# The token-major copy of x: whole transfers out, pieces of 512 bytes back, and a copy on ScalarE

## The chip, the cores and the metric

The kernel runs on one core of a Trainium2 chip. Its metric is the device time of one execution in microseconds (us); the time before is the median of three runs, 964.47 us. Work is spread over five engines that run side by side and wait for each other by semaphores: TensorE (PE, matrix products), VectorE (DVE), ScalarE (ACT), GpSimd (POOL) and SyncE (SP, which issues transfers). Transfers between device memory (DRAM) and the on-chip memory run on 16 DMA engines. Those that SP issues go into one queue (q1 in the profile), those that POOL issues into another (q0).

## The reference

Two decoder layers over 256 tokens of 1024 features, and a last normalization. Only the last block of layer 1, a feed-forward block, and the final normalization matter here:

```python
def rmsnorm(x, g):
    y = x32 * lax.rsqrt(jnp.mean(x32 * x32, axis=-1, keepdims=True) + EPS)
    return y.astype(x.dtype) * g

def swiglu(x, w_gate, w_up, w_down):
    return (jax.nn.silu(x @ w_gate) * (x @ w_up)) @ w_down

...
    x = x + 0.5 * swiglu(rmsnorm(x, ffn2_norm[l]), ffn2_w_gate[l], ffn2_w_up[l], ffn2_w_down[l])
return rmsnorm(x, final_norm)
```

w_gate and w_up are 1024 x 2816, w_down is 2816 x 1024. Everything is float32.

## The kernel before

**Stream of weights.** All weights come as one stream of 1 MB loads into four `raw` buffers (L117, issued by SP). PE multiplies float32 as a high and a low part, so each half of a load (a block of 128 x 1024) is split: ACT writes the high part `whi` (L143), DVE the low part `wlo` (L144). There are five buffers of each. A load can only be issued when its raw buffer, the one used four loads before, has been split; a block can only be split when PE is through with the block five before. Every product with a tile of weights is three matmuls (L579 to L581 for gate and up, L688 to L690 for a group that is made with seven products in the place of eight, L795 to L797 for the last down projection).

**x and its copy.** The residual x lies in on-chip memory with features on the partitions: a tile of 128 partitions x 8 feature groups x 256 tokens. The last block puts out tokens on the partitions, so it needs x turned. This is done through a DRAM tile `tok`, while PE works on gate and up. `to_tokens` (L508) is called four times, for two feature groups each: DVE transposes blocks of 32 x 32 (L513) into a tile `q`, and SP issues eight DMAs (L516) that put the pieces in their places of `tok`, which is 256 tokens x 1024 features. A run of 32 features is a piece, 128 bytes; a DMA moves 32 partitions x 8 pieces. `from_tokens` (L840) reads all of `tok` back with one DMA from POOL's queue (L842) into the tile `bias`, 128 partitions x 2 token halves x 1024 features, which `evac_tok` (L804) then uses: it adds half the down projection to it, takes the mean of squares, scales it, and the result goes out from there.

**What else runs there.** The hidden values are turned by `turned_back` (L544): POOL writes a tile `v`, `kT` or `k` to DRAM (L551) and reads it back with four DMAs (L553); ACT and DVE split what comes back into `h` (L561, L562). For the group with seven products, 1 MB loads with accumulation go from POOL's queue into the tiles `k2` and `bias` (L536, L633), and blocks are split from these too.

**Order.** `Order` (L200) holds a planned time of PE in nanoseconds; `pe.after(delay, fn, 0)` places `fn` at that planned time, in the order of the program. `to_tokens` is placed 16, 25, 34 and 43 us after the block's start, `from_tokens` 88 us after it. Each engine carries out its instructions in that order. SP holds the loads and the tok writes in one line, ACT the splits, the activations and everything else that is given to it.

Of the kernel before, what the change touches and what calls it, by code (L numbers as in the profile page):

```python
# [15 lines left out]
F32 = mybir.dt.float32  # L16
F32R = mybir.dt.float32r
AF = mybir.ActivationFunctionType
# [5 lines left out]
P = 128  # L24
D = 1024
KT = D // P
S = 256
# [213 lines left out]
def paired(t):  # L241

    return t.rearrange("p (b a) -> p a b", b=2)
# [22 lines left out]
def build(nc, tc, ctx, a):  # L266
    consts = ctx.enter_context(tc.tile_pool(name="consts", bufs=1))
    wpool = ctx.enter_context(tc.tile_pool(name="wpool", bufs=1))
    act = ctx.enter_context(tc.tile_pool(name="act", bufs=1))
    psum = ctx.enter_context(tc.tile_pool(name="psum", bufs=1, space=PSUM))  # L270
    dram = ctx.enter_context(tc.tile_pool(name="dram", bufs=1, space=DRAM))
# [13 lines left out]
    def w2():  # L285
        return act.tile([P, 512], F32, name="w2", bufs=6)
# [5 lines left out]
    x = consts.tile([P, KT, S], F32, name="x")  # L292
# [22 lines left out]
    pe = Order()  # L315
# [192 lines left out]
    def to_tokens(tok, k):  # L508


        to = tok.rearrange("(c i) (k p j) -> p k i c j", i=32, p=4, j=32)
        t = act.tile([P, 2 * S], F32, name="q2", bufs=2)
        tc.keep_in_program_order(nc.vector.transpose(t, x[:, k:k + 2].rearrange("p k s -> p (k s)")))  # L513
        for p in range(4):
            for i in range(2):
                tc.keep_in_program_order(nc.sync.dma_start(  # L516
                    to[p, k + i], t[32 * p:32 * p + 32, i * S:(i + 1) * S].rearrange("i (c j) -> i c j", j=32)))


    def placed(at):  # L520
        return [at + o // 2 + i for i, o in enumerate(PLACES)]
# [16 lines left out]
    def ffn(which, layer, n, nxt, first=False, last=False):  # L538
# [206 lines left out]
        def have(ks):  # L745
            return lambda: math.inf if any(h[k] is None for k in ks) else 0.0
# [26 lines left out]
        def down_tok():  # L773

            late = 2 * (ws.BUFS - 1)
            pss, got, mean = {}, {}, [EPS, EPS]

            def part(fs, *regions):  # L780

                c = regions[0][1] // 512

                def go():
                    for f in fs:
                        if (f, c) not in got:
                            got[f, c] = ws.take(f"{which}_w_down", layer, f * P, c * 512, 4)
                        for reg in regions:
                            u, c0, c1 = reg
                            if f == 0:  # L790
                                pss[reg] = (sc_tile if c == 1 and c1 - c0 == 512 else acc_tile)()[:, :c1 - c0]
                            ps = pss[reg]
                            wh, wl = (paired(w)[:, (c0 - c * 512) // 2:(c1 - c * 512) // 2] for w in got[f, c])
                            hh, hl = (h[f].v[:, u, m] for m in range(2))
                            nc.tensor.matmul(ps, hh, wh, start=f == 0, stop=False)  # L795
                            nc.tensor.matmul(ps, hh, wl, start=False, stop=False)  # L796
                            nc.tensor.matmul(ps, hl, wh, start=False, stop=f == FT - 1)  # L797
                    if fs[-1] == FT - 1:
                        for u, c0, c1 in regions:
                            evac_tok(u, slice(c0, c1), pss[u, c0, c1])  # L800

                return have(fs), go, sum(len(fs) * (c1 - c0) * 654 // 512 for _, c0, c1 in regions)

            def evac_tok(u, at, ps):  # L804
                xtok = back["x"]
                y = xtok[:, u, at]
                g = gfin[at.start // 512][:, at.start % 512:at.start % 512 + at.stop - at.start]
                nc.vector.scalar_tensor_tensor(y, ps, 0.5, y, op0=ALU.mult, op1=ALU.add)
                ms = act.tile([P, 1], F32, name="mean", bufs=4)
                junk = w2()[:, :at.stop - at.start]  # L810
                nc.vector.tensor_tensor_reduce(junk, y, y, 1.0 / D, mean[u], ALU.mult, ALU.add, ms)
                mean[u] = ms
                if at.stop < D:
                    nc.gpsimd.tensor_tensor(y, y, g, op=ALU.mult)
                    return
                r = act.tile([P, 1], F32, name="rcol", bufs=2)
                nc.gpsimd.tensor_tensor(r, ms, mhalf[:, 0:1], op=ALU.pow)
                nc.vector.tensor_tensor(y, y, g, op=ALU.mult)
                out = a["out"][u * P:(u + 1) * P]
                cuts = (0, 384, 704, D)  # L820
                nc.scalar.activation(xtok[:, u, :cuts[1]], xtok[:, u, :cuts[1]], AF.Copy, scale=r)
                nc.scalar.dma_start(out[:, :cuts[1]], xtok[:, u, :cuts[1]])
                for i, j in zip(cuts[1:], cuts[2:]):
                    nc.vector.tensor_scalar(xtok[:, u, i:j], xtok[:, u, i:j], r, None, op0=ALU.mult)
                    nc.sync.dma_start(out[:, i:j], xtok[:, u, i:j])

            end = range(FT - late, FT)
            right = ((0, 512, D), (1, 512, 768), (1, 768, D))
            return [part(range(i, i + 2), (0, 0, 512), (1, 0, 512)) for i in range(0, FT, 2)] + [
                part(range(FT - late), *right)] + [part(end, reg) for reg in right]  # L830
# [4 lines left out]
        norm_scale(n, 18900 if first else 2300, unpin=True, turn=not first, wide=False)  # L835
        if last:
            gfin = []
            tok, back = dram.tile([S, D], F32, name="tok"), {}

            def from_tokens():  # L840
                back["x"] = t = act.tile([P, 2, D], F32, name="bias", bufs=1)
                tc.keep_in_program_order(nc.gpsimd.dma_start(t, tok.rearrange("(u q) f -> q u f", u=2)))  # L842

            def last_factors():
                gfin.extend(act.tile([P, 512], F32, name="p2", bufs=4) for _ in range(2))
                src = a["final_norm"]
                for i, g in enumerate(gfin):
                    nc.sync.dma_start(g, bass.AP(tensor=src.tensor, offset=src.offset + i * 512, ap=[[0, P], [1, 512]]))

            pe.after(90000, last_factors, 0)  # L850
            for k in range(0, KT, 2):
                pe.after(16000 + 9000 * (k // 2), lambda k=k: to_tokens(tok, k), 0)
            pe.after(88000, from_tokens, 0)
        at = AT.get((which, layer))
        groups = [f0 for f0 in range(0, FT, 4) if at is None or f0 != SEVEN]
        ups = [f for f0 in groups for f in hidden(f0)]
# [504 lines left out]
    pe.after(60000, mem_scale, 0)  # L1361
    pe.after(100000, lambda: early.update(bias=load_bias(0)), 0)
    ffn("ffn1", 0, n, nxt, first=True)
    bias, sinks = early["bias"], (vecs[:, VCOL["sinks"]:VCOL["sinks"] + 8], nsinks)

# [11 lines left out]
    memory(0, n, nxt, keys[0])  # L1377
    n, nxt = nxt, xn(("ffn1_norm", 1))
    ffn("ffn2", 0, n, nxt)
    n, nxt = nxt, xn(("mix_norm", 1))  # L1380
    pe.after(114000, lambda: early.update(bias=load_bias(1)), 0)
    ffn("ffn1", 1, n, nxt)
    n, nxt = nxt, xn(("xa_norm", 1))
    odd_mixer(n, nxt, early["bias"], mem_keys(1))
# [73 lines left out]
```

## Time and profile before

| | us |
|---|---|
| runs | 965.64, 964.47, 962.23 (median 964.47) |
| the profiled execution's own time | 963.72 |
| its span, first to last instruction | 961.9 |
| mean granted TensorE clock | 0.994 |
| DMA: mean rate over the span | 245 GB/s |
| tok writes (L516): 32 issues of 32 KB, median from issue to landing | 6.4 |
| read of tok (L842): one issue of 1 MB, to landing | 11.6 |

The rows of the profile give an instruction's start and duration from the span's start, its engine and line, what it writes and reads, and, in square brackets, how long the engine had been idle before it and what ended that. The last feed-forward block begins about 776 us into the span; the tok writes are issued from 798.9 to 843.4 us, tok is read at 889.0 us, and the down projection runs from 897.4 us. "x2" behind a row means that two like instructions are merged in it.

### The profile page before, as it was taken

To read this page: it belongs to the slowest core of one execution; us is meant where nothing else is said; L and a number is where in the kernel's file an instruction comes from. 1 tells how busy PE (TensorE), PEld (TensorE's weight loads), DVE (VectorE), ACT (ScalarE), POOL (GpSimd) and SP (SyncE) were. 2 spreads that over 40 slices of the span, in tenths; PEclk is the share of its full clock that TensorE was granted. 3 is DMA by queue.
4 is the path that set the end of the run, shared out by engine and by line. 5 is a ranking of instruction groups with operands and counts; after the bars stand their busy time and mean duration, and the time that the engine had idled before them with its cause. 6 is when DMAs were issued, how large, how long until landed. Compare 5 with 4: busy or idle time off the path is not lost.

```text
span 961.9 us, 15192 instructions
## 1 busy us (share of the span) xinstructions
PE 948.4 (99%) x5796; PEld 868.7 (90%) x5796; DVE 726.5 (76%) x1153; ACT 594.1 (62%) x968; POOL 116.1 (12%) x204
## 2 busy tenths in 40 slices
PE   9999999999999999999999999999999999899997
PEld 8888899999999888889988888999999988688896
DVE  7667667788869877976777697677777889488583
ACT  7555555697658866555476655556875887265451
POOL 0411210001000111121001112100000010112121
PEclk9999999999999999999999999999999999989999
DMA  9999875555437899989759977855544479997841
GB/s 374 317 362 329 310 231 203 194 185 191 176 133 265 219 264 341 259 293 323 249 177 275 331 248 273 294 216 206 189 137 171 175 231 290 272 321 265 273 186 45
DMA packets 47450, 235.45 MB, mean 245 GB/s; under 512 B 14217, under 2 KB 15241, under 8 KB 22801
## 3 DMA queue, kind: packets, MB, share of 16 engines
q1 hardware_dynamic: 35056, 182.43, 52.2%
q0 software_dynamic: 11744, 51.42, 20.5%
q8 instruction: 45, 0.74, 0.3%
q10 hardware_dynamic: 576, 0.64, 0.2%
q14 instruction: 29, 0.23, 0.1%
HBM read 220.81 MB, written 16.80 MB: 247 GB/s over the span
## 4 chain that ended last, share of the span: by engine, by line
PE 94%; DMA 3%; DVE 2%; issue 0%; ACT 0%; POOLq 0%; DVEq 0%; ACTq 0%; SPq 0%
PE acc L580 11%; PE acc L581 11%; PE acc L579 11%; PE acc L418 8%; PE acc L423 7%; PE acc L425 7%; PE acc L424 7%; PE acc L419 4%; PE sc L418 3%; DMA raw<-in_w 2%; PE tr L689 2%; PE tr L688 2%; PE tr L690 2%; PE acc L797 2%; PE acc L796 1%; PE sc L419 1%
## 5 line engine op out<-in xcount | busy, mean ns | idle before, releaser
L144 DVE TENSOR_TENSOR wlo<-raw,whi 128x1024 fp32r<-128x1024 f32 (+2 forms) x363 | 409.6, 1140 | 154.6 <-ACT whi L143 152.2
L143 ACT ACTIVATE whi<-raw 128x1024 fp32r<-128x1024 f32 (+2 forms) x363 | 353.7, 986 | 244.7 <-PE acc L581 82.7
L580 PE MATMUL acc<-wlo,x 128*128 128x512 f32 x528 | 201.7, 382 | 0.6 <-DVE wlo L144 0.5
L579 PE MATMUL acc<-whi,x 128*128 128x512 f32 x528 | 196.5, 382 | 5.2 <-ACT whi L143 5.2
L581 PE MATMUL acc<-whi,x 128*128 128x512 f32 x528 | 200.7, 381 | 0.0
L579 PEld LDWEIGHTS acc<-whi,x 128*128 128x128 f32 x528 | 100.4, 190 | 20.1 <-ACT whi L143 5.9
L580 PEld LDWEIGHTS acc<-wlo,x 128*128 128x128 f32 x528 | 100.3, 190 | 16.6 <-DVE wlo L144 2.4
L581 PEld LDWEIGHTS acc<-whi,x 128*128 128x128 f32 x528 | 100.4, 190 | 14.1
L418 PE MATMUL acc<-h,whi 128*128 128x512 f32 x330 | 108.6, 382 | 0.0
L419 PE MATMUL acc<-h,wlo 128*128 128x256 f32 x330 | 90.0, 273 | 0.0
L425 PE MATMUL acc<-h,wlo 128*128 128x256 f32 x322 | 87.7, 275 | 0.0
L424 PE MATMUL acc<-h,whi 128*128 128x256 f32 x322 | 87.7, 275 | 0.0
L423 PE MATMUL acc<-h,whi 128*128 128x256 f32 x322 | 86.5, 277 | 0.0
L425 PE MATMUL acc<-x,wlo 128*128 128x256 f32 x304 | 84.1, 278 | 0.0
L424 PE MATMUL acc<-x,whi 128*128 128x256 f32 x304 | 83.8, 277 | 0.0
L423 PE MATMUL acc<-x,whi 128*128 128x256 f32 x304 | 83.3, 278 | 0.0
L418 PEld LDWEIGHTS acc<-h,whi 128*128 128x128 f32 x330 | 62.4, 189 | 8.6
L419 PEld LDWEIGHTS acc<-h,wlo 128*128 128x128 f32 x330 | 63.3, 192 | 0.2
L424 PEld LDWEIGHTS acc<-h,whi 128*128 128x128 f32 x322 | 61.7, 192 | 0.1
L425 PEld LDWEIGHTS acc<-h,wlo 128*128 128x128 f32 x322 | 61.7, 192 | 0.1
L423 PEld LDWEIGHTS acc<-h,whi 128*128 128x128 f32 x322 | 60.6, 192 | 0.4 <-DVE x L486 0.2
L424 PEld LDWEIGHTS acc<-x,whi 128*128 128x128 f32 x304 | 58.2, 192 | 0.2
(273 smaller groups left out, 1726.2 us busy)
## 6 DMA issues: line engine op xcount, KB each, us to landing
raw<-in_w SPq DMA_DIRECT2D x165, 1024.0 KB, 6.8
bias<-in_w POOLq DMA_DIRECT2D x12, 1024.0 KB, 11.0
k<-in_w POOLq DMA_DIRECT2D x9, 1024.0 KB, 9.2
turn<-v POOLq DMA_DIRECT2D x9, 512.0 KB, 3.3
v<-turn POOLq DMA_DIRECT2D x36, 128.0 KB, 7.1
dists<-line POOLq DMA_DIRECT2D x2, 1536.0 KB, 12.5
raw<-in_memT SPq DMA_DIRECT2D x3, 1024.0 KB, 4.7
turn<-kT POOLq DMA_DIRECT2D x6, 512.0 KB, 10.4
```

The costliest lines, as they stand in the source:

```text
L143: for ins in (self.nc.scalar.activation(hi[:, at], src, AF.Copy), self.nc.vector.tensor_tensor(lo[:, at], src, hi[:, at].bitcast(F32), op= ...
L144: self.nc.vector.tensor_tensor(lo[:, at], src, hi[:, at].bitcast(F32), op=ALU.subtract)):
L418: nc.tensor.matmul(ps, w[0], x2.both, start=start, stop=False)
L419: nc.tensor.matmul(ps[:, :S], w[1], x2.high, start=False, stop=stop)
L423: nc.tensor.matmul(ps[:, :S], w[0], x2.high, start=start, stop=False)
L424: nc.tensor.matmul(ps[:, :S], w[0], x2.low, start=False, stop=False)
L425: nc.tensor.matmul(ps[:, :S], w[1], x2.high, start=False, stop=stop)
L579: nc.tensor.matmul(ps[u], xh, wh, start=k == 0, stop=False)
L580: nc.tensor.matmul(ps[u], xh, wl, start=False, stop=False)
L581: nc.tensor.matmul(ps[u], xl, wh, start=False, stop=k == KT - 1)
L688: nc.tensor.matmul(ps, xh, wh, start=p == 0, stop=False)
L689: nc.tensor.matmul(ps, xh, wl, start=False, stop=False)
```

## The change

`tok` becomes 4 x 128 x 512, one plane for each call of `to_tokens`. The transpose writes its blocks in another order, so that the tile `q` is stored as it lies, with one DMA of 128 rows of 2 KB. Reading back takes four DMAs of POOL's queue, one for each block of 32 tokens in a half, with 32 partitions x 16 pieces of 512 bytes. What arrives in `bias` has the right token on each partition, but its features lie in blocks of 32 in another order, for both token halves. So ACT copies it in 16 steps of 128 x 128 (one for each feature group and token half) into a new tile, `k2`, in the natural order of features. `evac_tok` uses this one. `from_tokens` is placed at 93 us instead of 88, and the copies from 27 us after that.

```diff
     def to_tokens(tok, k):
-        to = tok.rearrange("(c i) (k p j) -> p k i c j", i=32, p=4, j=32)
         t = act.tile([P, 2 * S], F32, name="q2", bufs=2)
-        tc.keep_in_program_order(nc.vector.transpose(t, x[:, k:k + 2].rearrange("p k s -> p (k s)")))
-        for p in range(4):
-            for i in range(2):
-                tc.keep_in_program_order(nc.sync.dma_start(
-                    to[p, k + i], t[32 * p:32 * p + 32, i * S:(i + 1) * S].rearrange("i (c j) -> i c j", j=32)))
+        tc.keep_in_program_order(nc.vector.transpose(t.rearrange("q (a g j) -> q g a j", a=4, g=4),
+                                                     x[:, k:k + 2].rearrange("p k (u a i) -> p (k u) a i", u=2, a=4)))
+        tc.keep_in_program_order(nc.sync.dma_start(tok[k // 2], t))
...
-                xtok = back["x"]
+                xtok = back["y"]
...
-            tok, back = dram.tile([S, D], F32, name="tok"), {}
+            tok, back = dram.tile([KT // 2, P, 2 * S], F32, name="tok"), {}
             def from_tokens():
-                back["x"] = t = act.tile([P, 2, D], F32, name="bias", bufs=1)
-                tc.keep_in_program_order(nc.gpsimd.dma_start(t, tok.rearrange("(u q) f -> q u f", u=2)))
+                t = act.tile([P, 2 * D], F32, name="bias", bufs=1)
+                for b in range(4):
+                    tc.keep_in_program_order(nc.gpsimd.dma_start(
+                        t[32 * b:32 * b + 32].rearrange("i (g z) -> i g z", g=16),
+                        tok.rearrange("k (p i) (a z) -> a i (k p) z", p=4, a=4)[b]))
+                v = t.rearrange("q (k p m u j) -> q u k m p j", k=4, p=4, m=2, u=2)
+                def natural(k):
+                    y = back["y"] = back.get("y") or act.tile([P, 2, D], F32, name="k2", bufs=1)
+                    for u in range(2):
+                        nc.scalar.activation(y[:, u, k * P:(k + 1) * P].rearrange("q (p j) -> q p j", p=4),
+                                             v[:, u, k // 2, k % 2], AF.Copy)
+                for k in range(KT):
+                    pe.after(27000 + 1500 * k, lambda k=k: natural(k), 0)
...
-            pe.after(88000, from_tokens, 0)
+            pe.after(93000, from_tokens, 0)
```

The order of PE's and DVE's instructions stays as it was. On three engines rows are replaced or added. First SP, in the last feed-forward block, from the first tok write to the end; `raw<-in_w` are the weight loads. Before:

```order
L516 DMA tok<-q_8835 32x8x32 x8
L117 DMA raw<-in_w 128x2048 x2
L516 DMA tok<-q_8921 32x8x32 x8
L117 DMA raw<-in_w 128x2048
L516 DMA tok<-q_9000 32x8x32 x8
L117 DMA raw<-in_w 128x2048 x2
L516 DMA tok<-q_9092 32x8x32 x8
L117 DMA raw<-in_w 128x2048 x18
```

And now:

```order
L514 DMA tok<-q_8835 128x512
L117 DMA raw<-in_w 128x2048 x2
L514 DMA tok<-q_8914 128x512
L117 DMA raw<-in_w 128x2048
L514 DMA tok<-q_8986 128x512
L117 DMA raw<-in_w 128x2048 x2
L514 DMA tok<-q_9071 128x512
L117 DMA raw<-in_w 128x2048 x18
```

The loads stand where they stood; between them are now four writes in the place of 32. Where the texts below speak of loads A and B, these are the two between the third and the fourth group of writes, and C is the first of the 18.

Then POOL, where gate and up end; `k` is the turned tile of the hidden values, `turn` its place in DRAM. Before:

```order
L551 DMA turn<-k_9435 128x1024
L553 DMA k_9435<-turn 32x4x256 x4
L842 DMA bias<-tok 128x2x1024
L551 DMA turn<-kT 128x1024
L553 DMA kT<-turn 32x4x256 x4
```

And now:

```order
L547 DMA turn<-k_9407 128x1024
L549 DMA k_9407<-turn 32x4x256 x4
L839 DMA bias<-tok 32x16x128 x4
L547 DMA turn<-kT 128x1024
L549 DMA kT<-turn 32x4x256 x4
```

The read of tok keeps its place in the row, though its planned time is 5 us later; it is four issues now, ahead of the write of kT.

Last ACT, where the down projection begins; `whi<-raw` are splits of weight blocks, `h<-k` and `h<-kT` splits of turned hidden values. Before:

```order
L561 ACTIVATE h<-k_9435 128x2x128 x4
L143 ACTIVATE whi<-raw 128x1024
L611 ACTIVATE w_9683<-acc,rcol 128x256
L611 ACTIVATE w_9684<-acc,rcol 128x256
L143 ACTIVATE whi<-raw 128x1024 x3
L561 ACTIVATE h<-kT 128x2x128 x4
```

And now:

```order
L143 ACTIVATE whi<-raw 128x1024
L607 ACTIVATE w_9658<-acc,rcol 128x256
L607 ACTIVATE w_9659<-acc,rcol 128x256
L143 ACTIVATE whi<-raw 128x1024
L847 ACTIVATE k_9727<-bias 128x128 x16
L143 ACTIVATE whi<-raw 128x1024 x2
L557 ACTIVATE h<-kT 128x2x128 x4
```

The 16 copies stand in one piece behind the first of three splits, and the two other splits and those of kT wait behind them on ACT.

## The prediction

> **What bounds the kernel now.** I read the busy shares first, then the slices, to see whether TensorE (PE) ever stops.
>
> ```profile
> span 961.9 us, 15192 instructions
> PE 948.4 (99%) x5796; PEld 868.7 (90%) x5796; DVE 726.5 (76%) x1153; ACT 594.1 (62%) x968; POOL 116.1 (12%) x204
> PE   9999999999999999999999999999999999899997
> PEclk9999999999999999999999999999999999989999
> ```
>
> PE is busy 99% of the span. Only two slices show less before the end, one in PE and the next in the granted clock, around 841 us; the change sits in that feed-forward block. So anything off PE is worth something only through that hole, or by opening a new one. Next the timeline of PE there.
>
> ```profile
> 836.60 0.38 PE L581 MATMUL acc<-whi,x 128*128 128x512 f32 x1
> ...
> 842.15 0.79 PE L579 MATMUL acc<-whi,x 128*128 128x512 f32 x1 [5.17 <-ACT whi L143]
> 843.40 0.79 PE L580 MATMUL acc<-wlo,x 128*128 128x512 f32 x1 [0.47 <-DVE wlo L144]
> ...
> 848.15 0.38 PE L579 MATMUL acc<-whi,x 128*128 128x512 f32 x1
> ...
> 849.88 0.38 PE L581 MATMUL acc<-whi,x 128*128 128x512 f32 x1
> ```
>
> From 848.15 to 849.88 lie 8 starts, so at full pace one such product starts every 0.216 us. From 836.60 to 848.15 there are 13 steps, which would take 13 x 0.216 = 2.8 us and took 11.55. **The hole costs 8.75 us**: about 5.3 of waiting (836.82 to 842.15), the rest a slow restart, where the granted clock dips. Who is late is told by the chain of waits through the hole, and by a row of ACT's timeline.
>
> ```profile
> 815.22 5.78 DMA tok<-q
> ...
> 821.09 19.85 DMA raw<-in_w
> ...
> 841.04 1.06 ACT whi L143
> ...
> 842.13 1.24 DVE wlo L144
> ```
>
> ```profile
> 841.04 2.00 ACT L143 ACTIVATE whi<-raw 128x1024 fp32r<-128x1024 f32 x2 [13.33 <-DMA raw<-in_w]
> ```
>
> ACT sat 13.33 us without a weight block to split. Load A, issued at 821.09, took 19.85 us, and it was issued late because SP was still issuing the third group of writes into tok. Now the DMA view of 826 to 834 us (first three lines), the median landing of all loads after 770, and of those issued from 820 to 843.
>
> ```profile
> DMA packets 526, 1.99 MB, mean 249 GB/s; under 512 B 288, under 2 KB 288, under 8 KB 288
> q0 software_dynamic: 198, 1.36, 81.8%
> q1 hardware_dynamic: 327, 0.61, 21.5%
> ...
> raw<-in_w SPq DMA_DIRECT2D x27, 1024.0 KB, 7.2
> ...
> raw<-in_w SPq DMA_DIRECT2D x2, 1024.0 KB, 20.8
> ```
>
> q1 is SP's queue, q0 POOL's. In these 8 us POOL's accumulating loads (L633) hold the engines for 82%, while q1 passes 327 packets, 288 of them tiny: the 128-byte pieces of tok. Load A stands behind them in q1. About 3 q1 packets pass for 2 of q0, whatever their size, so a queue of many small packets crawls past large ones. A load takes 7.2 us normally, 20.8 here.
>
> **The change, part by part.** *Writes.* 32 transfers in 128-byte pieces (8,192 pieces) become 4 of 128 rows x 2 KB (512 rows). Each group of 8 also held SP:
>
> ```profile
> 815.22 5.76 SPq L516 DMA_DIRECT2D tok<-q  x8
> 821.09 1.30 SPq L117 DMA_DIRECT2D raw<-in_w  x2
> 822.77 20.94 SPq L516 DMA_DIRECT2D tok<-q  x8
> 843.81 79.84 SPq L117 DMA_DIRECT2D raw<-in_w  x18
> ```
>
> The last group kept SP from 822.77 to 843.7, so load C, the next, was issued at 843.81. With one issue per group SP is free after as long as one of them takes when nothing is in its way, and a load goes out when its buffer is free:
>
> ```profile
> 843.41 0.30 SPq L516 DMA_DIRECT2D tok<-q  x1
> ```
> There are four raw buffers, so A takes that of the load just before the first group, B and C those of the two loads between groups one and two. DVE finished with them here:
>
> ```profile
> 815.25 2.34 DVE L144 TENSOR_TENSOR wlo<-raw,whi 128x1024 fp32r<-128x1024 f32 x2
> 818.22 2.36 DVE L144 TENSOR_TENSOR wlo<-raw,whi 128x1024 fp32r<-128x1024 f32 x2 [0.62 <-ACT whi L143]
> ...
> 822.66 1.19 DVE L144 TENSOR_TENSOR wlo<-raw,whi 128x1024 fp32r<-128x1024 f32 x1
> ```
>
> So A can go at 817.6, B at 820.6, C at 823.9. PE runs dry at 836.8; each load feeds it for 5.2 us (24 products of 0.216), and ACT needs 1.06 first, so A must be there by 835.7, B by 840.9, C by 846.1. At the normal 7.2 us they land at 825, 828 and 831; even at 17 us each would be in time. I therefore take the whole hole out: **-8.75 us**. What is late next is then C, by this count 15 us early.
>
> *Transposes.* L513 writes its tile in another order, with strides. Nearest rows: the same operation with plain output, and L549, whose view on the output side is strided already.
>
> ```profile
> 822.03 0.71 DVE L513 STREAM_TRANSPOSE q<-x 128x512 f32<-128x512 f32 x1
> 830.21 0.70 DVE L549 STREAM_TRANSPOSE kT<-w 128x512 f32<-128x512 f32 x1
> ```
>
> 0.71 against 0.70: nothing, four times; neither end of that range reaches PE.
>
> *Read back and copies.* One 1 MB read (L842) becomes four of 32 partitions x 16 pieces of 512 bytes, and ACT then makes 16 copies of 128 x 128 (L847) between two blocks that it splits. The rows of POOL, ACT and PE there (PE's is the first product of the down projection):
>
> ```profile
> 886.83 2.19 POOL L553 DMA_DIRECT2D k<-turn  x4 [7.04 <-issue]
> 889.01 0.73 POOL L842 DMA_DIRECT2D bias<-tok  x1
> 890.89 0.57 POOL L551 DMA_DIRECT2D turn<-kT  x1 [1.16 <-DVE kT L549]
> ...
> 899.50 1.99 ACT L143 ACTIVATE whi<-raw 128x1024 fp32r<-128x1024 f32 x2
> 902.74 1.06 ACT L143 ACTIVATE whi<-raw 128x1024 fp32r<-128x1024 f32 x1 [1.25 <-PE acc L797]
> 911.97 1.33 ACT L561 ACTIVATE h<-kT 128x256 fp32r<-128x256 f32 x4 [8.17 <-DMA kT<-turn]
> ...
> 897.36 0.38 PE L795 MATMUL acc<-whi,h 128*128 128x512 f32 x1
> ```
>
> The copies come after the first of the two at 899.50, so at about 900.5 (in times of before). Their price: four of 128 x 256 take 1.33 us, 0.33 each, and the new ones are half as wide with the same runs of 32. Bounds: 16 x 0.33 = 5.3 us above, half of it, 2.7, below; I take 3.3, nearer the lower as the width is halved. What is behind them? The five whi buffers put ACT four blocks ahead: the block started at 902.74 waited until PE freed a buffer, so PE wants it 4 x 2.59 us later (12 products each), at 913.1, and the block delayed by the copies at 910.5. ACT and DVE need 1.06 + 1.2 us for it, so it must start by 908.2, and the copies by 904.9 (902.9 at 5.3 us). ACT idles 1.25 + 8.17 us just behind, which swallows 3.3 or 5.3: cost zero if the read has landed by 904.9. Without that cover the copies would cost their full 3.3 us.
>
> Does it land? The view of DMAs from 886 to 904 us:
>
> ```profile
> DMA packets 1103, 5.77 MB, mean 320 GB/s; under 512 B 144, under 2 KB 144, under 8 KB 656
> q1 hardware_dynamic: 494, 3.65, 54.2%
> ...
> bias<-tok POOLq DMA_DIRECT2D x1, 1024.0 KB, 11.6
> k<-turn POOLq DMA_DIRECT2D x4, 128.0 KB, 8.1
> ```
>
> The old read landed 11.6 us after 889.0, at 900.6. POOL's issues of this piecewise form (k<-turn, 1 KB pieces) take 2.19 / 4 = 0.55 us each, so the fourth is out at 891.2 where the one was at 889.7: about 902, as the bytes are the same. Pieces of 1 KB leave no packet between 512 B and 2 KB in this view, so that queue joins them; 512 bytes are not shown. Below: four that land sooner than 900.6 gain nothing, as ACT is not there yet. Above: at the pace of k<-turn (0.5 MB in 8.1 us) 1 MB takes 16.2 us and lands at 905.2, and with copies at 5.3 us that is 2.3 us too late. I take 902, by the nearest row (the same bytes, place and queue): **0 us**. turn<-kT behind them on POOL moves from 890.89 to 891.2; h<-kT is wanted for f = 16, at 897.4 + 16 x 1.29 = 918, and ACT ends it at 913.3 now: covered by over 4 us, less what the read loses in q0.
>
> Here the Trainium skill ("DMA: Bandwidth & Descriptors", Bandwidth) speaks against the split read: it wants transfers of 1 MiB or more, and its fit for this path ("Anatomy of one DMA", 2.0 us plus bytes at 436 GB/s) gives, as an estimate, four in series 10.4 us against 4.4 for one, 6 us later. By that rule the sum would come out as in the second rival below; the four k<-turn transfers, issued 0.55 us apart and landed 8.1 us after, overlap, and speak against it.
>
> The end (last products, norms, output) is the same work on another tile. Sum: 963.72 (the profiled execution's own time) - 8.75 + 0 = **955.0 us**. The median of the runs, 964.47, is 0.75 above the profiled one.
>
> **Rivals.** *The hole is only halved.* POOL's accumulating loads still fill q0 and the loads behind C come late. For it: 82% of q0 in the rows above. Against: q1's packets are then large and pass in turn. About half the hole: 963.7 - 4.4 = 959.3.
>
> *The read lands a few us late.* If the four go at k<-turn's pace, 16.2 us for 1 MB, and only from the last issue (890.7) on, they land at 906.9, the copies end at 910.2, and the block's low part is ready 2.3 us later, at 912.5, against 910.7: 1.8 us, and up to 3.4 more if PE restarts slowly: 956.8 to 960.2, say 958.0. For: more transfers in a queue beside one that loads fill to 54%. Against: the old read moved the same bytes in 11.6.
>
> *The hole has another cause.* If the accumulating loads alone delay A, nothing moves: 963.7. Against: A's wait behind tok's issues stands in the chain.
>
> *Slower: the pieces of 512 bytes travel one by one.* Place: q0 at 889 to 914. 2,048 packets at the 327 per 8 us that a queue passed beside a full one take 50 us if q1 is always full; q1 fills 54%, so about 25. The read lands at 914, copies end at 917.3, the wanted block is ready at 918.4 instead of 910.5: 7.9 us idle and 3.4 of slow restart, as in the hole (8.75 - 5.3): 963.7 - 8.75 + 11.3 = 966.3. It turns the sign from a landing near 911.5 on. Against: the joined 1 KB pieces. The Trainium skill (same page, "SWDGE vs HWDGE vs iDMA") says POOL's queue packs up to 4096 B preferably into a packet; by that rule this case falls away, and no run so far shows it for 512 bytes.
>
> **How the numbers follow.** Hole gone, no new one: 0.64 (954 to 956.5). Halved 0.17; late read 0.09; other cause 0.06; piecewise 0.04. A measurement tells about 0.3% (2.9 us) from no change. Faster: 0.64 + 0.16 + 0.08 = 0.88; same: 0.06 + 0.03 = 0.09; slower 0.03. The range runs from 953.0 (two us for spread, as the runs of before have) to 961.0 (the halved hole and its spread; the upper bounds of read and copies together, 2.3 + 3.4 of slow restart, give 960.7), leaving out the last two cases and tails.
>
> **What would show it.** Right: PE busy without a gap from 820 to 850, clock 1.00 there; loads after 817 landing in 7 to 10 us; SP's write issues one each; ACT's 16 copies in 3 to 5 us followed by idle time before h<-kT. Wrong: ACT waiting for raw near 830, or PE waiting for whi just after the copies (then the read's landing, above 16 us, says which rival).

## The result, and the profile after

| | median us | lowest to highest | runs |
|---|---|---|---|
| before | 963.97 | 962.23 to 965.64 | 5 |
| changed | 958.12 | 955.92 to 959.47 | 5 |

The ratio of the two is 0.9937, with a 95% interval from 0.9916 to 0.9959: the change is about 6 us faster. The prediction was 955.0, from 953.0 to 961.0. The profiled execution of the changed kernel took 956.50 us (before 963.72).

The page of the changed kernel, with the same lines as were read before:

```profile
span 954.5 us, 15174 instructions
...
PE 945.7 (99%) x5796; PEld 866.9 (91%) x5796; DVE 726.4 (76%) x1153; ACT 596.8 (63%) x984; POOL 118.0 (12%) x207
...
PE   9999999999999999999999999999999999999997
...
PEclk9999999999999999999999999999999999999999
```

The 8 in PE's row and the 8 in the granted clock are gone. The busy time of each engine in two stretches (the first is where the hole was, the second where the copies are; columns: length, PE, PEld, DVE, ACT, POOL, granted clock, DMA share, GB/s) shows that one place opened a little in exchange:

```profile
830.00:850.00 20.00, 20.00 (x94) 17.52 (x93) 11.65 (x15) 11.09 (x16) 2.62 (x5) 1.00 1.02 318
895.00:912.00 17.00, 16.31 (x76) 13.98 (x75) 9.89 (x14) 12.38 (x30) 4.92 (x9) 1.00 0.81 279
```

PE is busy for all of the first 20 us; in the second it misses 0.69.

**Where the hole was.** SP's timeline of the changed kernel:

```profile
814.88 0.33 SPq L514 DMA_DIRECT2D tok<-q  x1
817.72 3.31 SPq L117 DMA_DIRECT2D raw<-in_w  x2
822.87 0.33 SPq L514 DMA_DIRECT2D tok<-q  x1
823.98 91.88 SPq L117 DMA_DIRECT2D raw<-in_w  x18
```

A group of writes is one issue of 0.33 us, and the loads that the prediction called A and C go out at 817.72 and 823.98 (B, 3 us behind A, is merged into A's row). C had been issued at 843.81. But they do not land quickly. The view of DMAs from 817 to 845 us (queues with packets, MB and share of the engines; then the median time to landing of the loads):

```profile
q0 software_dynamic: 661, 3.82, 64.1%
q1 hardware_dynamic: 689, 3.81, 36.3%
...
raw<-in_w SPq DMA_DIRECT2D x6, 1024.0 KB, 17.3
```

17.3 us is over twice the 7.2 of an ordinary load, though no piece of tok in q1 is now below 2 KB: q1 has about as many packets and MB as q0 in this stretch, and little more than half its share of the engines. ACT's timeline shows how much of the room this used:

```profile
830.45 2.00 ACT L143 ACTIVATE whi<-raw 128x1024 fp32r<-128x1024 f32 x2 [2.63 <-DVE w L600]
837.84 2.00 ACT L143 ACTIVATE whi<-raw 128x1024 fp32r<-128x1024 f32 x2 [4.90 <-DMA raw<-in_w]
...
840.98 1.99 ACT L143 ACTIVATE whi<-k 128x1024 fp32r<-128x1024 f32 x2
...
847.20 2.00 ACT L143 ACTIVATE whi<-raw 128x1024 fp32r<-128x1024 f32 x2 [3.08 <-DMA raw<-in_w]
```

The first row is A's two blocks, the second B's, the last C's. ACT waits for B and for C. Between them two blocks of `k` come from POOL's queue. PE does not stop, but it is close; its own rows where it comes to C, and the low part of C's blocks on DVE:

```profile
849.65 0.38 PE L686 MATMUL tr<-whi,h 128*128 128x512 f32 x1
849.87 0.38 PE L575 MATMUL acc<-whi,x 128*128 128x512 f32 x1
850.09 0.38 PE L576 MATMUL acc<-wlo,x 128*128 128x512 f32 x1
```

```profile
848.29 2.36 DVE L144 TENSOR_TENSOR wlo<-raw,whi 128x1024 fp32r<-128x1024 f32 x2 [3.39 <-ACT whi L143]
```

The first of the two low parts is ready half of 2.36 us after 848.29, at 849.5, and the product that reads it starts at 850.09: 0.6 us to spare.

DVE, though, had stood 3.39 us for C and then worked without a break, so what comes behind is late. The same instruction before and in the changed kernel, and below it the write of `k` on POOL that follows from DVE's work:

```profile
859.65 0.68 DVE L727 TENSOR_TENSOR h<-h,tr 128x512 f32<-128x512 f32 x1
853.06 0.68 DVE L723 TENSOR_TENSOR h<-h,tr 128x512 f32<-128x512 f32 x1
```

```profile
879.22 0.56 POOL L551 DMA_DIRECT2D turn<-k  x1 [3.37 <-DVE k L549]
872.62 0.56 POOL L547 DMA_DIRECT2D turn<-k  x1 [3.43 <-DVE k L545]
```

Both come only 6.6 us earlier than before, while the work that follows PE comes 8.64 us earlier (ACT's blocks at 884.61 before and 875.97 now, for one): DVE and POOL are 2.0 us behind, and this reaches the read of tok.

**Where the copies are.** POOL, and ACT below it, in the changed kernel:

```profile
880.30 2.19 POOL L549 DMA_DIRECT2D k<-turn  x4 [7.12 <-ACT whi L143]
882.48 2.59 POOL L839 DMA_DIRECT2D bias<-tok  x4
887.47 0.57 POOL L547 DMA_DIRECT2D turn<-kT  x1 [2.40 <-DMA k<-turn]
899.06 2.19 POOL L549 DMA_DIRECT2D kT<-turn  x4 [11.01 <-ACT k L847]
```

```profile
892.15 1.06 ACT L143 ACTIVATE whi<-raw 128x1024 fp32r<-128x1024 f32 x1
897.16 3.31 ACT L847 ACTIVATE k<-bias 128x128 f32<-128x128 f32 x16 [3.96 <-DMA bias<-tok]
900.38 1.99 ACT L143 ACTIVATE whi<-raw 128x1024 fp32r<-128x1024 f32 x2
```

ACT stands 3.96 us in front of the copies, waiting for the read of tok; they then take 3.31 us, and the block behind them starts at 900.38. PE's timeline shows the end of that chain, and the chain of waits names its beginning:

```profile
901.67 0.38 PE L791 MATMUL acc<-whi,h 128*128 128x512 f32 x1
902.74 0.48 PE L792 MATMUL acc<-wlo,h 128*128 128x512 f32 x1 [0.69 <-DVE wlo L144]
903.06 0.38 PE L793 MATMUL acc<-whi,h 128*128 128x512 f32 x1
```

```profile
884.42 12.64 DMA bias<-tok
```

From 901.67 to 903.06 are two steps of 0.216 us, and they took 1.39: 0.96 us lost. The last of the four pieces of the read was issued at 884.42 and landed 12.64 us later, 14.6 us after the first issue.

### The profile page after: what moved, and what is told of

Read it like the earlier page. It is cut to its first block, busy times and chain, and to the rows that moved or that the text cites. A ratio compares the mean times of both kernels' runs of the same rounds, so it can differ in the third digit from the quotient of the medians.

```text
span 954.5 us, 15174 instructions
## 1 busy us (share of the span) xinstructions
PE 945.7 (99%) x5796; PEld 866.9 (91%) x5796; DVE 726.4 (76%) x1153; ACT 596.8 (63%) x984; POOL 118.0 (12%) x207
## 4 chain that ended last, share of the span: by engine, by line
PE 95%; DMA 2%; ACT 1%; DVE 0%; POOL 0%; issue 0%; POOLq 0%; SPq 0%; DVEq 0%; ACTq 0%
PE acc L576 11%; PE acc L577 11%; PE acc L575 11%; PE acc L418 8%; PE acc L423 7%; PE acc L425 7%; PE acc L424 7%; PE acc L419 4%; PE sc L418 3%; PE tr L685 2%; PE tr L684 2%; PE tr L686 2%; PE sc L575 2%; PE sc L576 2%; PE sc L577 2%; PE sc L419 2%
## 6 DMA issues: line engine op xcount, KB each, us to landing
bias<-in_w POOLq DMA_DIRECT2D x12, 1024.0 KB, 12.6
```

## The experiments

Every kernel was timed beside the kernel before on the same chip; three groups ran, with medians of 964.91, 963.91 and 964.31 for the kernel before. Runs of one kernel here spread over 1 to 9 us, so differences below 2 us between single medians are weak.

**The changed kernel again**, as the yardstick of the first and the third group, with no edit.

> The changed kernel again, as the measure for the other runs on this chip, with a second profile. First theory (the hole is gone and the rest of the forecast gain is lost where ACT waits for the read of tok): 956 to 959 us, PE idle about 0.7 us near 902 and nowhere near 837. Rival (the loads beside POOL's accumulating loads land so late that PE still stops in some executions): the same time, but with an idle stretch of PE between 835 and 850 in some profiles, and loads landing 17 us or more after issue there.

> The changed kernel, as the measure for the next run on the same chip: 956 to 959 us.

Measured: 958.02 (955.05 to 960.88), ratio 0.9928 [0.9905, 0.9950], and 958.24 (956.90 to 961.40), ratio 0.9934 [0.9912, 0.9956]. The first one's profiled execution was its longest, 960.88, and shows where it lost time. PE's and ACT's timelines:

```profile
902.78 0.48 PE L791 MATMUL acc<-whi,h 128*128 128x512 f32 x1 [0.87 <-ACT whi L143]
904.04 0.48 PE L792 MATMUL acc<-wlo,h 128*128 128x512 f32 x1 [0.78 <-DVE wlo L144]
...
918.95 0.48 PE L791 MATMUL acc<-whi,h 128*128 128x512 f32 x1 [1.44 <-ACT whi L143]
920.21 0.48 PE L792 MATMUL acc<-wlo,h 128*128 128x512 f32 x1 [0.78 <-DVE wlo L144]
```

```profile
898.48 3.30 ACT L847 ACTIVATE k<-bias 128x128 f32<-128x128 f32 x16 [4.70 <-DMA bias<-tok]
...
917.23 0.72 ACT L557 ACTIVATE h<-v 128x256 fp32r<-128x256 f32 x2 [6.96 <-DMA v<-turn]
```

Two places make up most of it. At 902.78 the copies were late, as above but by more. At 918.95 ACT had stood 6.96 us in front of `h<-v`, and since it works in order, the next block's split came too late. `v` comes through POOL's queue behind the read: its write went out 2.3 us later than in the first profile (903.52 and 901.23), and the write and the reads back then took 5.3 and up to 6.2 us, where they had taken 2.8 and up to 3.6. So the late read is felt by the copies and explains a part of v's delay; why v's own transfers were slower is not known.

The table takes the steps between PE's starts that are longer than 0.216 us and adds up what they have too much, in two stretches of each profiled execution (the two steps above at 901.67 to 903.06 give the 0.96 of the change; before has the prediction's 8.75). The last column is the profiled time less both.

| profiled execution | us | lost 825 to 870 | lost 895 to 925 | us less losses |
|---|---|---|---|---|
| before | 963.72 | 8.75 | 0 | 955.0 |
| the change | 956.50 | 0 | 0.96 | 955.5 |
| after_again | 960.88 | 0 | 5.39 | 955.5 |
| after_third | 959.41 | 0 | 4.00 | 955.4 |
| w_only | 956.62 | 0 | 1.28 | 955.3 |
| small_pieces | 960.99 | 1.14 | 4.01 | 955.8 |
| eight_issues | 961.64 | 3.23 | 3.32 | 955.1 |
| copies_later | 959.68 | 0 | 3.87 | 955.8 |
| no_copies | 960.40 | 0 | 4.14 | 956.3 |
| read_earlier | 956.14 | 0 | 0.84 | 955.3 |
| read_later | 955.30 | 0 | 0 | 955.3 |
| four_whole | 955.84 | 0 | 0.70 | 955.1 |
| pieces_out | 956.26 | 1.25 | 0 | 955.0 |
| pieces_out_again | 955.58 | 0.42 | 0 | 955.2 |

The last column moves by 1.3 us, from 955.0 to 956.3, where the times move by 8.4: these two stretches hold nearly all there is to explain. Of the 4.00 us of after_third about 1.7 are not waiting: after PE had stood near 903, its granted clock was 0.57 from 904 to 908 us and its steps took 0.43 us in place of 0.216, a slow restart as in the hole of the kernel before.

**w_only: the writes alone.** tok is written as in the change, read back whole by one transfer, and not copied.

```diff
-                for b in range(4):
-                    tc.keep_in_program_order(nc.gpsimd.dma_start(
-                        t[32 * b:32 * b + 32].rearrange("i (g z) -> i g z", g=16),
-                        tok.rearrange("k (p i) (a z) -> a i (k p) z", p=4, a=4)[b]))
...
-                for k in range(KT):
-                    pe.after(27000 + 1500 * k, lambda k=k: natural(k), 0)
+                tc.keep_in_program_order(nc.gpsimd.dma_start(
+                    t, tok.rearrange("k (p i) z -> (k p i) z", p=4).rearrange("(q r) z -> q (r z)", r=4)))
+                back["y"] = t.rearrange("q (u f) -> q u f", u=2)
```

> Only the writes of the change: tok is read back by one whole 1 MB transfer, and ACT's 16 copies are left out (so the features stay in the wrong order). First theory: ACT no longer waits for 512-byte pieces nor copies, the rest of the gain comes back: 954 to 956 us, 2 to 3 under the changed kernel. Rival (late loads): within 1 us of the changed kernel, 957 to 959.

Measured: 956.53 (956.08 to 957.25), ratio 0.9914 [0.9897, 0.9932]. That is 8.4 us below the kernel before of its group, and 1.5 below the change, with runs that lie within 1.2 us. POOL's timeline shows what is different there:

```profile
881.77 2.18 POOL L549 DMA_DIRECT2D k<-turn  x4 [8.91 <-issue]
883.94 0.57 POOL L838 DMA_DIRECT2D bias<-tok  x1
884.51 0.55 POOL L547 DMA_DIRECT2D turn<-kT  x1
895.14 2.21 POOL L549 DMA_DIRECT2D kT<-turn  x4 [10.08 <-ACT whi L143]
```

turn<-kT follows the read at once, 3 us earlier than in the change, although k<-turn began later. The read itself landed 9.4 us after its issue. So the new writes are worth 8.4 us. That the piecewise read with its copies takes some 1.5 back is likely by the medians, but the two intervals overlap, and the two profiled executions do not show it: that of w_only lost 1.28 us near 915, where `h<-v` waited 6.69 us for v, that of the change 0.96.

**small_pieces and eight_issues: the two halves of the hole.** The first keeps one issue per group and cuts it into pieces of 128 bytes; the second keeps the rows and divides each group into eight issues of 32 rows of 1 KB.

```diff
-        tc.keep_in_program_order(nc.sync.dma_start(tok[k // 2], t))
+        tc.keep_in_program_order(nc.sync.dma_start(tok[k // 2].rearrange("(c a) (b j) -> (a b) c j", c=16, j=32),
+                                                   t.rearrange("p (c j) -> p c j", j=32)))
```

> The changed kernel with its four writes of 256 KB as they are, but each in pieces of 128 bytes (16 for each partition, put 128 rows apart; so tok's order is wrong). If the size of the packets in q1 made the hole: loads land 20 us or more after issue near 820, PE stops near 837 again, 961 to 964 us. If the number of issues made it (eight to a group keep SP from issuing loads): no hole, 957 to 959 as the change.

```diff
-        tc.keep_in_program_order(nc.sync.dma_start(tok[k // 2], t))
+        for p in range(4):
+            for i in range(2):
+                rows, half = slice(32 * p, 32 * p + 32), slice(i * S, (i + 1) * S)
+                tc.keep_in_program_order(nc.sync.dma_start(tok[k // 2, rows, half], t[rows, half]))
```

> The changed kernel with each of the four writes cut into eight issues of 32 partitions x 1 KB (the order in tok is right). If the size of the packets made the hole: no hole, 957 to 959. If the number of issues made it: SP is kept from issuing loads for 15 us or more around 825, PE stops near 837, 961 to 964.

Measured: small_pieces 960.35 (958.84 to 965.29), ratio 0.9962 [0.9947, 0.9976]; eight_issues 961.64 (959.66 to 963.70), ratio 0.9970 [0.9957, 0.9983]. The change in the same group was 958.24: 2.1 and 3.4 us less (the interval of the first overlaps with the change's, that of the second just clears it). In small_pieces A and B go out on time, and a group is one issue of 0.38 us. But the pieces hold SP all the same: the issue of C, behind the last group, took 18.19 us, where it takes 0.33 in the change, though DVE was done with its buffer at 824.21. What held it the profile does not tell. ACT then waits longer for C than in the change (5.64 us to 3.08), and PE runs dry for a moment:

```profile
824.24 18.19 SPq L117 DMA_DIRECT2D raw<-in_w  x1
```

```profile
848.89 2.00 ACT L143 ACTIVATE whi<-raw 128x1024 fp32r<-128x1024 f32 x2 [5.64 <-DMA raw<-in_w]
```

```profile
851.26 0.48 PE L577 MATMUL acc<-wlo,x 128*128 128x512 f32 x1 [0.75 <-DVE wlo L144]
```

In eight_issues the tiny pieces are gone and the last group still holds SP. Its timeline, and the row of SP's waits from 822 to 843 us (total, times, longest):

```profile
820.45 0.85 SPq L117 DMA_DIRECT2D raw<-in_w  x2
822.62 19.31 SPq L517 DMA_DIRECT2D tok<-q  x8
843.66 1.94 SPq L117 DMA_DIRECT2D raw<-in_w  x4
```

```profile
SPq L517 <- DMA raw<-in_w: 14.5, 2, 7.4
```

```profile
842.81 0.48 PE L578 MATMUL acc<-whi,x 128*128 128x512 f32 x1 [0.79 <-ACT whi L143]
```

SP spends 14.5 of these 19.31 us waiting for two loads to land before it may issue a *write*. The program gives each issuing engine eight completion semaphores in turn, so an issue has to wait until the transfer issued eight before has landed: the seventh write goes out at 834.20, and A, eight issues before it, landed at 834.18; the eighth goes out at 841.63, and B landed at 841.61. C then goes out at 843.66, as late as in the kernel before. Yet PE loses 3.2 us and not 8.75.

The landings tell why (each load's issue and landing in us, and the hole):

| | A | B | C | lost 825 to 870 |
|---|---|---|---|---|
| before | 821.09, 840.93 | 821.69, 843.39 | 843.81, 849.39 | 8.75 |
| eight_issues | 820.45, 834.18 | 820.91, 841.61 | 843.66, 850.01 | 3.23 |
| small_pieces | 817.98, 828.27 | 820.97, 835.68 | 824.24, 848.81 | 1.14 |
| the change | 817.72, 830.35 | 820.71, 837.76 | 823.98, 847.12 | 0 |

C lands within 0.6 us of 849.4 in the first three. In small_pieces A and B land no later than in the change, and nearly all of the 1.14 us are C's. In the other two A and B are late as well: they are issued up to 3.4 us later, behind the third group, and in the kernel before, where that group is in pieces of 128 bytes, A lands another 6.8 us later than in eight_issues. Neither half alone brings the hole back: 1.1 and 3.2 us where both together cost 8.75. The halves are not clean, as the pieces also make issues slow. In the kernel before, three writes of the last group took 3.07, 3.67 and 9.55 us to issue, 16.3 of the 20.94 in which SP was held, and only 2.1 were waiting for a load to land.

**copies_later and no_copies: is it the copies?** In the first the copies are spread between later splits, and held to that place in ACT's order; in the second the piecewise read stays and they are left out.

```diff
-                    pe.after(27000 + 1500 * k, lambda k=k: natural(k), 0)
+                    pe.after(34000 + 1500 * k, lambda k=k: natural(k), 0)
```

> The 16 copies are placed 7 us later and pinned, so they stand between later splits of ACT instead of in one piece; transfers unchanged. First theory: ACT's wait for the read (3.96 us in the profile of the change) goes, PE's 0.69 us near 902 with it, 0.7 to 3 us under the changed kernel. Rival (late loads): within 0.7 us of the changed kernel.

```diff
-                for k in range(KT):
-                    pe.after(27000 + 1500 * k, lambda k=k: natural(k), 0)
+                back["y"] = t.rearrange("q (u f) -> q u f", u=2)
```

> The changed kernel without ACT's 16 copies (so the features stay in the wrong order); the read in pieces stays. If ACT's wait for the read and the copies themselves cost the time: 956.5 us with narrow runs. If the read in q0 costs it by delaying the turned kT and v behind it: 957.5 to 959, runs spread over 3 us, PE idle between 905 and 925 us.

Measured: copies_later 960.29 (958.25 to 963.79), ratio 0.9957 [0.9938, 0.9975]; no_copies 960.70 (956.92 to 963.85), ratio 0.9965 [0.9950, 0.9980]. Neither is faster than the change; both medians are above it, with intervals that touch or overlap. No time came back when the copies were moved or left out, but a new wait stands in their place, so these two runs do not price the copies by themselves. ACT's timeline of no_copies:

```profile
908.52 1.34 ACT L557 ACTIVATE h<-kT 128x256 fp32r<-128x256 f32 x4 [9.12 <-DMA kT<-turn]
```

With the copies gone, or out of the way, ACT runs ahead and stands in front of `h<-kT` for 9.12 us (8.90 in copies_later), and the blocks behind that come late: PE loses 4.14 us from 895 to 925. The transfers of kT<-turn land here in 6.7 us, in the change in 2.9. A reading of this, not tested: where ACT stops early for its copies, raw buffers come free later, q1 carries less just then (53.7% of the engines from 897 to 912 in the change, 60.9% here), and POOL's transfers pass sooner.

no_copies shows something else. w_only has no copies either, and differs from it in the read alone: 0.9914 [0.9897, 0.9932] against 0.9965 [0.9950, 0.9980], intervals that do not overlap. Without copies, then, the read in four piecewise issues costs 4 to 5 us more than one whole read.

**read_earlier and read_later: the read at another place**, 23 us sooner, where its latency can't matter to the copies, and behind kT<-turn, so that it holds up neither turn<-kT nor kT<-turn. In both the copies are held to their place in ACT's order.

```diff
-                    pe.after(27000 + 1500 * k, lambda k=k: natural(k), 0)
+                    pe.after(50000 + 1500 * k, lambda k=k: natural(k), 0)
...
-            pe.after(93000, from_tokens, 0)
+            pe.after(70000, from_tokens, 0)
```

> The read of tok is placed 23 us earlier (ahead of POOL's write of the turned v), the copies about where they are, pinned. First theory: the read has landed long before the copies, no wait on ACT: 954.5 to 956 us. Rival (late loads): 957 to 959, or slower, as 1 MB more is asked of the DMA engines at about 855 to 870 us where loads are scarce.

```diff
-                    pe.after(27000 + 1500 * k, lambda k=k: natural(k), 0)
+                    pe.after(29000 + 1000 * k, lambda k=k: natural(k), 0)
...
-            pe.after(93000, from_tokens, 0)
+            pe.after(101000, from_tokens, 0)
```

> The read of tok is placed behind the write and the read of the turned kT on POOL's queue, and the copies behind ACT's split of kT (pinned). If the delay of kT in q0 and ACT's wait are the cost: 956 to 957 us. If the delay only moves on to the turned v, which now stands behind the read: 958 to 961.

Measured: read_earlier 958.14 (955.65 to 964.33), ratio 0.9938 [0.9916, 0.9960]; read_later 959.93 (955.30 to 963.63), ratio 0.9949 [0.9932, 0.9966]. Neither gains. The profiled executions (956.14 and 955.30) lie below these medians and lost little (0.84 and 0), so what makes the medians was not seen, and both are inconclusive on the mechanism. What is behind the read in read_later is turn<-v, and it landed in 11.0 us there, where it took 2.8 in the change.

**four_whole: four issues, but whole rows.** It separates the number of issues from the size of the pieces.

```diff
-                        t[32 * b:32 * b + 32].rearrange("i (g z) -> i g z", g=16),
-                        tok.rearrange("k (p i) (a z) -> a i (k p) z", p=4, a=4)[b]))
+                        t[32 * b:32 * b + 32], tok.rearrange("k (p i) z -> (k p i) z", p=4).rearrange(
+                            "(q r) z -> q (r z)", r=4)[32 * b:32 * b + 32]))
```

> The changed kernel, but each of the four reads of tok takes 32 whole rows of 8 KB instead of 32 x 16 pieces of 512 bytes (so the rows arrive in the wrong order); copies as in the change. If the size of the pieces is what makes the read slow, it lands in about 9.4 us as one whole read does, and the time is about 956.5 us. If four issues are what costs (POOL's write of kT is then issued only after k<-turn has landed, at 887.5 instead of 884.5 us), the time stays at 957.5 to 959 with runs spread over 3 us or more.

Measured: 956.46 (955.25 to 959.47), ratio 0.9924 [0.9906, 0.9943]. The four transfers of the read take 10.1 us by their median, in the change 10.9; from the first issue to the last landing it is 13.5 us, in the change 14.6. turn<-kT is still late:

```profile
881.42 1.98 POOL L839 DMA_DIRECT2D bias<-tok  x4
887.14 0.56 POOL L547 DMA_DIRECT2D turn<-kT  x1 [3.74 <-DMA k<-turn]
```

So the wait of turn<-kT belongs to the number of issues: with four for k<-turn and four for the read, turn<-kT is the ninth, and by the eight semaphores waits for the first k<-turn. What the pieces cost is not settled: the read lands only 1.1 us sooner without them, and the interval overlaps with the change's.

**pieces_out: the pieces on the other side.** The writes go out as four issues per group with pieces of 512 bytes, so that the read is one whole transfer; the copies stay, held to their place in ACT's order.

```diff
-        tc.keep_in_program_order(nc.sync.dma_start(tok[k // 2], t))
+        for p in range(4):
+            tc.keep_in_program_order(nc.sync.dma_start(
+                tok.rearrange("(a i) (g z) -> g i a z", a=4, g=16)[2 * k + p],
+                t[32 * p:32 * p + 32].rearrange("i (a z) -> i a z", a=4)))
...
+                tc.keep_in_program_order(nc.gpsimd.dma_start(t, tok))
```

> The pieces of 512 bytes are moved to the writes (4 issues of 32 partitions x 4 pieces for each pair of feature groups, 16 in all on SP), and tok is read back by one whole transfer; copies at the same place, pinned. If whatever is gained by the whole read is not lost again on SP's queue: 956.5 us, 1.5 under the change. If pieces of 512 bytes hold up the loads in q1 as those of 128 bytes did: a hole of PE near 837 again, 958 to 963.

> The version with the pieces in the writes and one whole read, beside the change on one chip: 955 to 957 us, 1.5 to 3 under the change, if the whole read is what it gains by; within 0.5 us of it if the difference between two chips or chance showed it before.

Measured: 955.45 (954.92 to 959.60), ratio 0.9917 [0.9898, 0.9936], and again 955.84 (955.11 to 959.84), ratio 0.9915 [0.9895, 0.9935]. In the same group as the second, the change took 958.24: 2.4 us more, with intervals that overlap; its three medians, 958.02 to 958.24, are all above the two of pieces_out. ACT's timeline of the first:

```profile
893.53 3.30 ACT L847 ACTIVATE k<-bias 128x128 f32<-128x128 f32 x16
...
900.87 1.34 ACT L560 ACTIVATE h<-kT 128x256 fp32r<-128x256 f32 x4 [2.15 <-DMA kT<-turn]
```

The copies take their 3.30 us without a wait in front of them, turn<-kT goes out right behind the read (884.26), and PE loses nothing after 895. The writes now cost a little at the other place, 1.25 and 0.42 us near 851, where loads land just late. Its two medians are the lowest of all kernels run here. It beats the kernel before; that it beats the change is likely, but not clear of the spread.

## Why the prediction was right, and where it was not

**The hole: right.** "I therefore take the whole hole out: -8.75 us". PE had no gap from 830 to 850, and the writes alone gave 8.4 us. Both causes that the prediction named, SP held by its own issues and tiny pieces in front of the loads, are needed for the whole of it, as small_pieces and eight_issues show. The prediction did not say how they share it, nor that the pieces hold SP too (18.19 us for one issue in small_pieces). Its "About 3 q1 packets pass for 2 of q0, whatever their size" is the mix of those 8 us and no fixed ratio: from 826 to 834 us in the changed kernel 158 packets of q1 passed to 161 of q0.

**The loads' landing: mis-sized, felt later.** The issue times were as forecast (817.6 and 823.9, measured 817.72 and 823.98), but the normal 7.2 us were 12.6, 17.1 and 23.1 for A, B and C: landings at 830.3, 837.8 and 847.1. The deadlines were 835.7, 840.9 and 846.1. C's was missed by 1.0, and PE did not stop, since two blocks of `k` lie between B and C, which the count left out, and PE came to C only at 849.87. "C, by this count 15 us early" was 0.6 us early by the rows above. PE did not feel it there, but DVE did, and with it POOL: turn<-k went out 2.0 us late, and the read of tok 2.1. So the rival of the halved hole, in which loads come late although the pieces are gone, was much closer to the event than its place in the forecast suggests: where C's split began at 848.89 (small_pieces) in place of 847.20, PE had a gap, and pieces_out shows a small one too.

**Transposes and copies: right.** The copies took 3.31 us (forecast 3.3), and PE had no loss at the transposes.

**The read: this step failed.** The sum took "about 902, as the bytes are the same", 13 us after the first issue, and 0 us. The profile of after runs 8.64 us ahead of that of before at this place (ACT's block at 889.79 there is at 881.15 here), so 902 is 893.4, and the limit for the copies, 904.9, is 896.3. The read landed at 897.06; the copies began at 897.16, 0.9 us too late, and PE lost 0.96. Two terms were too small: the first issue was at 882.48 and not 880.4 (889.0 in times of before), 2.1 us late from DVE, and the read took 14.6 us and not 13. By this count the copies would have been in time with only one of the two. The forecast for the profiled execution would have been 963.72 - 8.75 + 0.96 = 955.9, measured 956.50; 0.6 is unexplained. Over many runs the term looks larger, some 1.5 us by the medians of the change and w_only, and single profiles of the change lose 0.96, 4.00 and 5.39. That is the mechanism and nearly the price of the rival "the read lands a few us late" (958.0, measured 958.12), which got 0.09. The hole was right and the read too cheap; the range held because that rival was in it. That its price, 958.0, came so close to the median is partly luck: the one execution whose read is shown above took 956.50.

**What the read's step overlooked.** "turn<-kT behind them on POOL moves from 890.89 to 891.2" counted issue time alone. Before, in times of after, it stood at 882.25; now it is at 887.47, 5.2 us later: 2.1 as k<-turn starts later, 2.4 for the wait on k<-turn, the rest longer issues. The trace of before had a small sign of that wait on SP, the 2.1 us in which a write waited for a load, and the prediction did not carry it over to POOL. In the first profile `h<-kT` had room enough for that, as the prediction said; in after_again it was `v`, further back in the same queue, for which ACT stood 6.96 us.

**The split read as a rule.** The prediction weighed the Trainium skill ("DMA: Bandwidth & Descriptors", Bandwidth and "Anatomy of one DMA") against the k<-turn rows and sided with the rows. The direction of the rule held: the split read took 14.6 us from its first issue, whole ones of the same bytes 9.4 (w_only) to 11.6 (before), so 3.0 to 5.2 more; as an estimate the fit had said 6. What the Trainium skill says of packing pieces (same page, "SWDGE vs HWDGE vs iDMA") fits 512 bytes too. The view of DMAs from 882 to 898 us in the changed kernel has no packet between 512 bytes and 2 KB:

```profile
DMA packets 987, 4.53 MB, mean 283 GB/s; under 512 B 179, under 2 KB 179, under 8 KB 691
```

So the slow rival, pieces that travel one by one, fell as forecast.

**What stays open:** why leaving the copies out does not make the kernel faster (only argued above), how the read's cost divides between the number of issues, the pieces and the later turn<-kT, what kept SP in the 18.19 us of one issue, and what the executions of read_earlier and read_later above their medians waited for, as only one below it was profiled of each.

## What to carry to other kernels

Ask two things of each transfer in a queue of large ones: how many issues it takes, since in a program like this one an issue has to wait for the transfer issued eight before on that engine, and how small its pieces are, since here they delayed both the landing of the loads behind them and SP's next issue. If a layout must be cut into pieces somewhere, cut on the side that has slack, and let the side on which an engine waits in order be one whole transfer: here the medians of that version were about 2 us lower, which is likely a gain but not clear of the spread. And after an improvement, recount the margins with the landing times of that very stretch, not with a usual one: three of the loads took 12.6 to 23.1 us where the median elsewhere is 7.2. A load that is late on one engine can show up 35 us later on another, as C did through DVE in the read of tok.

## What was not expected of the hardware

- Large plain loads beside POOL's accumulating loads are slow with no piece below 2 KB in their queue: 17.3 us for 1 MB from 817 to 845, with 689 packets in q1 to 661 in q0, and 36.3% to 64.1% of the engines.
- The same 1 MB in four transfers of 512-byte pieces took 14.6 us from its first issue, though its packets were joined to 2 KB and more, and in four transfers of whole rows 13.5 (four_whole); one whole transfer took 9.4 (w_only), 9.7 and 11.2 (the two of pieces_out) and 11.6 (before).
- Behind one transfer of 2,048 pieces of 128 bytes, SP's issue of a 1 MB load took 18.19 us (small_pieces), where it took 0.33 behind the same bytes in rows of 2 KB.
- Taking work off an engine did not make the kernel faster: without the 3.3 us of copies on ACT the median was 960.70, and the transfers of kT<-turn took 6.7 us in place of 2.9.
